# A decoder layer's output projection: norms two column steps sooner, the FFN's last input norm inside its first unit, the table load behind the first down weights

## The chip, the cores and the metric

The kernel runs on one core of a Trainium2 chip. The time is that of one execution on the device, in microseconds (us); before and after are compared by medians over several executions.

## The reference

One decoder layer over 2048 prompt tokens and 32 sample tokens (2080 columns), in float32, D_MODEL 1024, D_FF 2688. The part that bears on the change is the end of the layer:

```python
    merged = jnp.concatenate([_rmsnorm(attn, p['g_attn']), _rmsnorm(ssm, p['g_ssm'])], axis=-1)
    x = x + merged @ p['w_out']
    f, conv_new = _conv_ffn(_rmsnorm(x, p['norm_ffn']), conv_prev,
                            p['w_up'], p['conv_w'], p['conv_b'], p['w_down'])
    x = x + f

def _conv_ffn(h, prev, w_up, conv_w, conv_b, w_down):
    L = h.shape[1]
    up = h @ w_up
    buf = jnp.concatenate([prev.astype(up.dtype), up], axis=1)
    c = conv_b + sum(conv_w[i] * buf[:, i:i + L] for i in range(CONV_W))
    a, g = jnp.split(c, 2, axis=-1)
    return (jax.nn.silu(g) * a) @ w_down, buf[:, -(CONV_W - 1):]
```

A final rmsnorm follows. `_rmsnorm` scales each token by the inverse root of its mean square, and by a weight per channel.

## The kernel before, in words

Channels lie on the partitions, tokens along the free axis. A float32 product is computed as three matmuls on two halves of each operand: `split` (L81) casts the high half on ScalarE (ACT) and subtracts it for the low half on VectorE (DVE) or GpSimd (POOL); `mm3` (L90) multiplies high by high, low by high and high by low (L92 to L94). Names that end in h and l are those halves.

*Output projection* (stage "wo"). `TILES3` cuts the columns into eight tiles of 260, numbered `it`. In each, eight output blocks `m` are made of 24 matmuls of 260 columns. A block's residual is loaded into a tile `xm` (12 buffers), DVE adds the PSUM sum to it (L1160), and it is written to the scratch `x2scr`. Four PSUM banks ("mm") hold block sums, two ("st") hold statistics. Between the blocks stand the norms of the tiles on either side. `merged_sums` loads the next tile's attention and SSM outputs (`mt`) and sums their squares; `merged_norm` makes its normalised halves mh and ml, by way of `mf` (two buffers, DVE), ACT's cast and POOL's subtraction. `rstd` (L97) does the scale: a matmul with ones (st_m, st_f), Ln and Exp on ACT, and three operations on DVE (L107 to L110). After block 2, `ffn_norm` normalises the tile before for the FFN: eight DVE products (L1128) into `h2` (three buffers), each written to the scratch `h2scr`. `early_sums` in tiles 5 and 6 and `begin_ffn` prepare FFN inputs from it.

*FFN.* It runs in two groups of columns (gi 0 and 1) of 21 units (j). A unit multiplies two up-weight blocks with the group's inputs x0, t2, q1 and q0 in 168 matmuls of 262 columns, as products ux, u2, s2, u3, s3, u4, s1: some sums are formed ahead of the product (q1, t2 and q0 are such sums of inputs), and some partial sums serve two outputs, for which ACT copies the running bank (`ca`, `cb`) before TensorE adds on. `conv` does the depthwise convolution and the gate, and writes the result `cc` to `actscr`. After a group's units stands `down` (L1419), the down projection in column tiles `TILESD`: `load_a` loads halves ah and al from `actscr`, `load_wd` (L1399) the raw weights wdr (four buffers), which are split into wdh and wdl. `prepare(1)` splits the second group's inputs beside the first `down`; `finish` and `last_norm` do the final rmsnorm.

*What sets the order.* TensorE's (PE) order is that of the code (`manual_schedule`). The other engines' order is made by a scheduler at build time. All loads and stores are issued by SyncE (SP) in one queue, in order. `after_preload` (L641) puts the ACT table load for Ln and Exp at a place in ACT's order, and holds back what is written inside it until that load; the FFN's Silu uses another table. Before, the whole of `down` stands inside one.

Of the kernel before, what the change touches and what calls it, by code (L numbers as in the profile page):

```python
# [18 lines left out]
P = 128  # L19
# [608 lines left out]
def body(tc, a):  # L628
# [16 lines left out]
    with ExitStack() as top:  # L645
# [399 lines left out]
        for tok in ORDER.split():  # L1045
            if tok == "Y":
                after_s5()
            elif tok == "T":
                steps["g"] = start_glu()
            elif tok == "M":  # L1050
                with after_preload():
                    st.norm = merged_norm(0, *st.sums, PS, "w")
                    st.ms_close()
            elif tok == "A":
                psw_close()
                psa_close()
                psg, psg_close = psum("p2pg", 4)
                st.glups = psg
                att_close()
                kvp_close()  # L1060
                ha, ha_close = pool("fha", "left")
                wop, wo_close = pool("wo", "left")
                for m in range(3, KD):
                    load_wo(m, wop, *[(nc.scalar, nc.vector, nc.gpsimd)[e] for e in WOE[m - 3]])
            else:
                next(steps[tok])
# [47 lines left out]
        with after_preload():  # L1114
            st.gl2_close()
            st.gl_close()
            p3b, p3b_close = pool("p3b", "left")
            st.p3o = p3b
            stg, stg_close = pool("stg", "left", 2)
# [3 lines left out]
            def ffn_norm(it, xs, ss):  # L1123
                t0, n = TILES3[it]
                r = rstd(c, p3b, pst, "st", ss, n, ones[1024], f"f_{it}")
                for k in range(KD):
                    h = p3b.tile([P, n], F32, tag="h2", name=f"h2_{it}_{k}", bufs=3)
                    nc.vector.scalar_tensor_tensor(h, xs[k], g_ffn[:, k : k + 1], r, ALU.mult, ALU.mult)  # L1128
                    nc.sync.dma_start(h2scr[:, k, t0 : t0 + n], h)

            def begin_ffn():
# [8 lines left out]
                for sub in range(2):  # L1140
                    t2 = ffn.t2[sub] = hi_lo(ffn.hc, [4, W], f"t2{sub}", 0)
                    for k in range(0, 4, 2):
                        s = ffn.c2.tile([P, 2, W], F32, tag="c2", name=f"t2r_{sub}_{k}")
                        nc.sync.dma_start(s, t2scr[:, sub, k : k + 2])
                        split(nc, *[t[:, k : k + 2] for t in t2], s, nc.scalar, (nc.vector, nc.gpsimd)[k // 2])

            old = None
            for it, (t0, n) in enumerate(TILES3):
# [5 lines left out]
                for m in range(KD):  # L1154
# [7 lines left out]
                    xs.append(xm)  # L1162
                    if it + 1 < len(TILES3):
                        if m == 0:
                            sums = merged_sums(it + 1, p3m)
                        if m == 3:
                            nxt = merged_norm(it + 1, *sums, pst, "st")
                    if m == 2 and old is not None:
# [5 lines left out]
                old = (it, xs, sumsq(c, p3b, xs, n, f"f_{it}", nc.vector))  # L1174
            ffn_norm(*old)
        ps_close()
        pst_close()
        psj_close()


        sp, up, c2 = ffn.sp, ffn.up, ffn.c2
        p3b_close()
        wo_close()
        hb, hb_close = pool("fhb", "left")
        xp, xp_close = pool("fxo", "left")
        psx, psx_close = psum("fpx", 4)
        psu, psu_close = psum("fpu", 2)
        psv, psv_close = zip(*[psum(f"fpv{i}", 1) for i in range(2)])

# [9 lines left out]
        def load_sums(gi, sub):  # L1199

            q1, t2 = ffn.q1[sub], ffn.t2[sub] = hi_lo(hb, [2, 4, W], f"q1{sub}", gi), hi_lo(ffn.hc, [4, W], f"t2{sub}", gi)
            for k in range(4):
# [15 lines left out]
        def load_wup(gi, j):  # L1218

            lo_eng = nc.vector if gi == 0 and j == 0 else nc.gpsimd  # L1220
            raws = []
# [29 lines left out]
        def load_q(i):  # L1251
            for sub in range(2):
                q = (ffn.q0, ffn.q1)[i][sub] = hi_lo(hb, [2, 4, W], f"q{i}{sub}", 0)
                for k in range(4):
                    s = c2.tile([P, 2, W], F32, tag="c2", name=f"q{i}r_{sub}_{k}")
                    nc.sync.dma_start(s, qscr[:, sub, i, k])
                    split(nc, *[t[:, :, k] for t in q], s, nc.scalar, (nc.gpsimd, nc.vector)[k % 2])

# [119 lines left out]

        def finish(t0, n, xs):

            ss = sumsq(c, DP, xs, n, f"fo_{t0}", nc.vector)
            yield
# [16 lines left out]
        def load_wd(gi, j, t0):  # L1399
# [5 lines left out]
            if gi and j < 14:  # L1405
                if j in (4, 5):
                    w = [ffn.hc.tile([P, D], F32R, tag=f"t2{j - 4}{i}", name=f"wd{i}_{j}") for i in "hl"]
                else:
                    i = j if j < 4 else j - 6
                    pl, nm = ((ha, "x0"), (hb, "q1"), (hb, "q0"))[0 if j < 4 else 1 + i // 4]  # L1410
                    t = pl.tile([P, 2, D], F32R, tag=f"{nm}{i % 4 // 2}{'hl'[i % 2]}", name=f"wd_{j}")
# [7 lines left out]
        def down(gi, beside):  # L1419

            old = None
            for ti, (t0, n) in enumerate(TILESD[gi]):
# [18 lines left out]
                for i, j in enumerate(order):  # L1441
                    for ahead in range(i, min(i + 3, NF)):
                        if ahead not in hls:
# [19 lines left out]
                for m in range(KD):  # L1463
# [3 lines left out]
                    with tc.high_priority(offset=HPD):  # L1467
                        nc.vector.tensor_tensor(x, x, pts[m][:, :n], ALU.add)  # L1468
                old = finish(t0, n, xs)
                next(old)  # L1470
# [10 lines left out]
        def last_norm():  # L1481
            with after_preload():
                next(old, None)

        old = None
        for gi in range(2):
            for j in range(NF):
                if (gi, j) != (0, 0):
                    ws = load_wup(gi, j)
                unit(gi, j, ws, None if j else last_norm if gi else lambda: load_q(0))  # L1490
            with after_preload():
                beside = prepare(1) if gi == 0 else iter(())
                old = down(gi, beside)
                for _ in beside:
                    pass
                if gi:
                    next(old, None)
        nc.sync.dma_start(a["o_tail"][:, :, 0:2], tailp)
        xp_close()
        hb_close()  # L1500
        ha_close()
        ffn.hc_close()
        ffn.c2_close()
# [117 lines left out]
```

## Time and profile before

| | us |
|---|---|
| median of 3 executions (lowest to highest) | 2224.45 (2221.5 to 2226.35) |
| the profiled execution | 2223.61 |
| its span in the profile | 2221.8 |
| TensorE busy | 2067.9 (93%) |
| DVE, POOL, ACT busy | 1330.2, 1192.1, 1058.9 |

The profiled execution was granted a mean TensorE clock of 0.965 of full speed. In the profile's rows L12 is line 12 of the kernel. A timeline row has the start and the length in us, engine, line, operation and tiles, written from source to target with "<-"; a bracket at its end is the idle time ahead of it on that engine and what ended it. A row of a group has the count, the busy time in us and the mean in ns of one, and the idle time ahead. A DMA row has the transfer, the count, its size and the median time in us from issue to landing.

### The profile page before, as it was taken

The page shows a single profiled execution, that of the slowest core. Times are in us where ns is not written, and L with a number is a line of the kernel's source. Part 1 is how long each engine was busy: PE and PEld are TensorE (multiplying, and loading weights), DVE is VectorE, ACT ScalarE, POOL GpSimd, SP SyncE. Part 2 cuts the span into 40 slices and gives each one's busy share as a digit, 9 for nine tenths or more (in the row PEclk, how much of TensorE's full clock was granted, in tenths as well). Part 3 has the DMA queues.
Part 4 walks back from the last instruction along what each step waited for, and adds up shares of the span by engine and source line. Part 5 has one row for each costly group of instructions (what it writes and reads, how often), then busy time and mean ns, then how long its engine had stood idle before and what let it go on. Part 6 is the DMA issues. An engine that isn't in the chain of part 4 may idle for free.

```text
span 2221.8 us, 41548 instructions
## 1 busy us (share of the span) xinstructions
PE 2067.9 (93%) x14685; PEld 1933.8 (87%) x14685; DVE 1330.2 (60%) x3328; ACT 1058.9 (48%) x2459; POOL 1192.1 (54%) x1166
## 2 busy tenths in 40 slices
PE   8969999978998979999999899999999999899997
PEld 7967878857988979999999687788999999888997
DVE  8859898457567766676667532417666666601231
ACT  6525554674443356666666432225556656532111
POOL 4857776334454456666665453555666666372211
PEclk9979999989999879999999899999999999999999
DMA  7855434685577752333333684844233333393643
GB/s 233 252 148 156 123 108 129 128 239 157 170 225 229 237 185 90 116 108 104 102 108 112 215 291 153 284 154 153 96 109 108 97 105 106 107 260 129 202 132 97
DMA packets 294352, 347.59 MB, mean 156 GB/s; under 512 B 42344, under 2 KB 250864, under 8 KB 294128
## 3 DMA queue, kind: packets, MB, share of 16 engines
q1 hardware_dynamic: 294144, 344.94, 51.1%
q8 instruction: 116, 1.90, 0.4%
q14 instruction: 92, 0.75, 0.1%
HBM read 232.70 MB, written 107.80 MB: 153 GB/s over the span
## 4 chain that ended last, share of the span: by engine, by line
PE 73%; DVE 7%; DMA 6%; issue 6%; POOL 3%; ACT 3%; SPq 2%; DVEq 0%; POOLq 0%; ACTq 0%
PE ux L1317 21%; PE u L1317 16%; PE dn L94 7%; PE dn L93 7%; PE dn L92 7%; PE qkv L92 2%; PE qkv L94 1%; PE qkv L93 1%; SPq L776 1%; PE o L541 1%; PE tp_b L530 1%; POOL ml L87 1%; PE wo L93 1%; PE wo L94 1%; PE wo L92 1%
## 5 line engine op out<-in xcount | busy, mean ns | idle before, releaser
L87 POOL TENSOR_TENSOR wdl<-wdr,wdh 128x1024 fp32r<-128x1024 f32 x65 | 159.7, 2464 | 270.3 <-ACT wdh L84 263.6
L92 PE MATMUL dn<-ah,wdh 128*128 128x512 f32 (+3 forms) x552 | 204.5, 370 | 15.0 <-ACT wdh L84 10.7
L94 PE MATMUL dn<-ah,wdl 128*128 128x512 f32 (+3 forms) x552 | 204.8, 371 | 3.2 <-POOL wdl L87 3.2
L93 PE MATMUL dn<-al,wdh 128*128 128x512 f32 (+3 forms) x552 | 204.6, 371 | 0.5 <-DMA al<-actscr 0.5
L1468 DVE TENSOR_TENSOR xo<-xo,dn 128x512 f32<-128x512 f32 (+3 forms) x40 | 21.9, 584 | 302.2 <-PE dn L94 302.1
L1282 ACT ACTIVATE cc<-u,cw 128x260 f32<-128x260 f32 (+1 forms) x252 | 141.5, 563 | 98.4 <-DVE u L1356 68.9
L84 ACT CAST wdh<-wdr 128x1024 fp32r<-128x1024 f32 x65 | 68.0, 1049 | 232.1 <-PE dn L93 208.9
L87 POOL TENSOR_TENSOR wls<-s,whs 128x1024 fp32r<-128x1024 f32 x41 | 98.8, 2411 | 133.4 <-ACT whs L84 133.4
L1283 DVE SCALAR_TENSOR_TENSOR cc<-u,cw,cc 128x260 f32<-128x260 f32 (+1 forms) x252 | 120.8, 480 | 62.4 <-ACT cc L1282 61.0
L93 PE MATMUL wo<-ml,wo 128*128 128x260 f32 x512 | 150.9, 295 | 7.2 <-POOL ml L87 7.0
L92 PE MATMUL wo<-mh,wo 128*128 128x260 f32 x512 | 152.2, 297 | 2.2 <-ACT mh L84 2.2
L94 PE MATMUL wo<-mh,wo 128*128 128x260 f32 x512 | 149.1, 291 | 0.0
L92 PEld LDWEIGHTS dn<-ah,wdh 128*128 128x128 f32 x552 | 104.7, 190 | 33.3 <-ACT wdh L84 11.3
L1356 DVE TENSOR_TENSOR u<-u,cb 128x262 f32<-128x262 f32 x84 | 36.4, 434 | 159.0 <-PE u L1317 159.0
L92 PE MATMUL qkv<-hh_p,wqh 128*128 128x256 f32 (+1 forms) x384 | 114.4, 298 | 12.1 <-DVE vs L879 8.2
L94 PEld LDWEIGHTS dn<-ah,wdl 128*128 128x128 f32 x552 | 104.5, 189 | 21.4 <-POOL wdl L87 5.1
L87 POOL TENSOR_TENSOR wlt<-s,wht 128x512 fp32r<-128x512 f32 x41 | 53.0, 1292 | 127.2 <-ACT wht L84 65.5
L93 PEld LDWEIGHTS dn<-al,wdh 128*128 128x128 f32 x552 | 104.8, 190 | 17.8 <-DMA al<-actscr 1.0
L1284 DVE SCALAR_TENSOR_TENSOR cc<-u,cw,cc 128x260 f32<-128x260 f32 (+1 forms) x252 | 119.4, 475 | 0.8
L87 POOL TENSOR_TENSOR wlg<-wur,whg 128x1024 fp32r<-128x1024 f32 x41 | 98.7, 2407 | 25.6 <-ACT whg L84 25.6
L93 PE MATMUL qkv<-hl_p,wqh 128*128 128x256 f32 (+1 forms) x384 | 111.0, 289 | 0.0
L94 PE MATMUL qkv<-hh_p,wql 128*128 128x256 f32 (+1 forms) x384 | 110.8, 289 | 0.0
(573 smaller groups left out, 8367.6 us busy)
## 6 DMA issues: line engine op xcount, KB each, us to landing
actscr<-cc SPq DMA_DIRECT2D x168, 260.0 KB, 4.7
wur<-in_w_up SPq DMA_DIRECT2D x84, 512.0 KB, 3.3
wdr<-in_w_down SPq DMA_DIRECT2D x77, 512.0 KB, 5.2
x<-in_xT SPq DMA_DIRECT2D x56, 256.0 KB, 3.8
hs<-h2scr SPq DMA_DIRECT2D x44, 262.0 KB, 4.9
ah<-actscr SPq DMA_DIRECT2D x42, 256.0 KB, 3.8
al<-actscr SPq DMA_DIRECT2D x42, 256.0 KB, 4.6
mt<-mscr SPq DMA_DIRECT2D x16, 520.0 KB, 5.3
```

The lines of the kernel that those rows point to most:

```text
L84: nc.scalar.copy(hi, src)
L87: lo_eng.tensor_tensor(lo, src, hi.bitcast(F32), ALU.subtract)
L92: nc.tensor.matmul(ps, w[0], x[0], start=first, stop=False)
L93: nc.tensor.matmul(ps, w[0], x[1], start=False, stop=False)
L94: nc.tensor.matmul(ps, w[1], x[0], start=False, stop=last)
L530: nc.tensor.transpose(tp[:, P * j : P * j + P], ss[kv][:, j, P * ch : P * ch + P], c.ident)
L541: nc.tensor.matmul(o_ps[64 * kv : 64 * kv + 64, :], vt[:, 64 * kv : 64 * kv + 64], pts[kv, ch], start=(ch == 0), stop=(ch == 1))
L1282: nc.scalar.activation(cp, pp[:, 2:], AF.Identity, bias=w[3], scale=w[2])
L1283: nc.vector.scalar_tensor_tensor(cp, pp[:, 1 : npr + 1], w[1], cp, ALU.mult, ALU.add)
L1284: nc.vector.scalar_tensor_tensor(cp, pp[:, 0:npr], w[0], cp, ALU.mult, ALU.add)
L1317: nc.tensor.matmul(pt[:, :W], x[p][:, k], y[q][:, k], start=start and k + i == 0, stop=k == 3 and i == 2, skip_group_check=True)
L1356: v.tensor_tensor(c21[s], c21[s], cb[s][:, 0], ALU.add)
```

## The change

It does four things. `merged_norm` is called after block 1 of a tile (block 3 in tile 0) and `merged_sums` after block 5 of the tile before that. `ffn_norm` writes in place into `xm` and has no h2 tiles. The last `ffn_norm`, some pools and the loading of q0 stand in a function `finish_front`, which runs in the middle of unit (0,0); q1 has a pool of its own (`hd`), and DVE makes all low halves of t2 and q1, POOL those of the first unit's weights. And `down` no longer stands inside `after_preload`: only the first tile's final sums of squares do. ah and al are loaded four ahead instead of three.

```diff
-            p3b, p3b_close = pool("p3b", "left")
-            st.p3o = p3b
+            st.p3o, p3o_close = pool("p3o", "left")
...
                 for k in range(KD):
-                    h = p3b.tile([P, n], F32, tag="h2", name=f"h2_{it}_{k}", bufs=3)
+                    h = xs[k]
                     nc.vector.scalar_tensor_tensor(h, xs[k], g_ffn[:, k : k + 1], r, ALU.mult, ALU.mult)
                     nc.sync.dma_start(h2scr[:, k, t0 : t0 + n], h)
...
                     xs.append(xm)
-                    if it + 1 < len(TILES3):
-                        if m == 0:
-                            sums = merged_sums(it + 1, p3m)
-                        if m == 3:
-                            nxt = merged_norm(it + 1, *sums, pst, "st")
+                    if m == 0 and it == 0:
+                        sums = merged_sums(1, p3m)
+                    if m == (1 if it else 3) and it + 1 < len(TILES3):
+                        nxt = merged_norm(it + 1, *sums, pst, "st")
+                    if m == 5 and it + 2 < len(TILES3):
+                        sums = merged_sums(it + 2, p3m)
                     if m == 2 and old is not None:
...
-            ffn_norm(*old)
         ps_close()
...
+        hd, hd_close = pool("fhd", "right")
         psx, psx_close = psum("fpx", 4)
         psu, psu_close = psum("fpu", 2)
-        psv, psv_close = zip(*[psum(f"fpv{i}", 1) for i in range(2)])
+
+        def finish_front():
+
+            nonlocal hb, xp, psv, hb_close, xp_close, psv_close
+            with after_preload():
+                ffn_norm(*old)
+            pst_close()
+            p3b_close()
+            hb, hb_close = pool("fhb", "left")
+            xp, xp_close = pool("fxo", "left")
+            psv, psv_close = zip(*[psum(f"fpv{i}", 1) for i in range(2)])
+            load_q(0)
+
+        hb = xp = psv = hb_close = xp_close = psv_close = None
...
-            q1, t2 = ffn.q1[sub], ffn.t2[sub] = hi_lo(hb, [2, 4, W], f"q1{sub}", gi), hi_lo(ffn.hc, [4, W], f"t2{sub}", gi)
+            q1, t2 = ffn.q1[sub], ffn.t2[sub] = hi_lo(hd, [2, 4, W], f"q1{sub}", gi), hi_lo(ffn.hc, [4, W], f"t2{sub}", gi)
...
-            lo_eng = nc.vector if gi == 0 and j == 0 else nc.gpsimd
+            lo_eng = nc.gpsimd
...
-                q = (ffn.q0, ffn.q1)[i][sub] = hi_lo(hb, [2, 4, W], f"q{i}{sub}", 0)
+                q = (ffn.q0, ffn.q1)[i][sub] = hi_lo((hb, hd)[i], [2, 4, W], f"q{i}{sub}", 0)
                 for k in range(4):
                     s = c2.tile([P, 2, W], F32, tag="c2", name=f"q{i}r_{sub}_{k}")
                     nc.sync.dma_start(s, qscr[:, sub, i, k])
-                    split(nc, *[t[:, :, k] for t in q], s, nc.scalar, (nc.gpsimd, nc.vector)[k % 2])
+                    split(nc, *[t[:, :, k] for t in q], s, nc.scalar, nc.vector if i else (nc.gpsimd, nc.vector)[k % 2])
...
-                    for ahead in range(i, min(i + 3, NF)):
+                    for ahead in range(i, min(i + 4, NF)):
...
-            with after_preload():
-                next(old, None)
-
-        old = None
+            next(last, None)
+
         for gi in range(2):
             for j in range(NF):
                 if (gi, j) != (0, 0):
                     ws = load_wup(gi, j)
-                unit(gi, j, ws, None if j else last_norm if gi else lambda: load_q(0))
-            with after_preload():
-                beside = prepare(1) if gi == 0 else iter(())
-                old = down(gi, beside)
-                for _ in beside:
-                    pass
-                if gi:
-                    next(old, None)
+                unit(gi, j, ws, None if j else last_norm if gi else finish_front)
+            beside = prepare(1) if gi == 0 else iter(())
+            last = down(gi, beside)
+            for _ in beside:
+                pass
+        next(last, None)
```

In the order, SP in tile 4 of the projection: xm_4_4 to xm_4_7 are the residuals of blocks 4 to 7, h2_3 the FFN's input from tile 3.

```order
L1129 DMA h2scr_64<-h2_3_0_9812 128x260
L1129 DMA h2scr_64<-h2_3_1_9815 128x260
L1129 DMA h2scr_64<-h2_3_2_9818 128x260
L1161 DMA x2scr_63<-xm_4_3_9836 128x260
L1156 DMA xm_4_4_9935<-in_xT 128x260
L1156 DMA xm_4_5_9964<-in_xT 128x260
L1129 DMA h2scr_64<-h2_3_3_9821 128x260
L1129 DMA h2scr_64<-h2_3_4_9824 128x260
L1156 DMA xm_4_6_9993<-in_xT 128x260
L1129 DMA h2scr_64<-h2_3_5_9827 128x260
L1156 DMA xm_4_7_10022<-in_xT 128x260
L1156 DMA xm_5_0_10074<-in_xT 128x260
```

```order
L1129 DMA h2scr_64<-xm_3_0_9315 128x260
L1129 DMA h2scr_64<-xm_3_1_9344 128x260
L1129 DMA h2scr_64<-xm_3_2_9443 128x260
L1129 DMA h2scr_64<-xm_3_3_9499 128x260
L1129 DMA h2scr_64<-xm_3_4_9528 128x260
L1129 DMA h2scr_64<-xm_3_5_9557 128x260
L1129 DMA h2scr_64<-xm_3_6_9612 128x260
L1129 DMA h2scr_64<-xm_3_7_9641 128x260
L1156 DMA xm_4_4_9906<-in_xT 128x260
L1156 DMA xm_4_5_9935<-in_xT 128x260
L1156 DMA xm_4_6_9990<-in_xT 128x260
L1156 DMA xm_4_7_10019<-in_xT 128x260
```

The sources of the h2scr writes are now xm tiles, and all eight stand ahead of the load of xm_4_4, which takes the buffer of xm_3_0.

TensorE at the end of the projection and the start of the FFN (wo_7_7 is the last block, st_f_7 the statistics of the last tile, ux, u3 products of unit 0):

```order
L93 MATMUL wo_7_7_11225<-ml_7_6_10766,wo07_8108 128x260
L94 MATMUL wo_7_7_11225<-mh_7_6_10765,wo17_8109 128x260
L92 MATMUL wo_7_7_11225<-mh_7_7_10771,wo07_8108 128x260
L93 MATMUL wo_7_7_11225<-ml_7_7_10772,wo07_8108 128x260
L94 MATMUL wo_7_7_11225<-mh_7_7_10771,wo17_8109 128x260
L101 MATMUL st_f_7_11275<-ss_f_7_11252,ones1024_77 128x260
L1317 MATMUL ux_0_0_0_11407<-x00h_0_8872,whv_0_0_11339 128x262
```

```order
L1328 MATMUL ux_0_0_1_11310<-t21l_0_10908,whs_0_0_11250 128x262
L1328 MATMUL ux_0_0_1_11310<-t21h_0_10907,wls_0_0_11251 128x262
L101 MATMUL st_f_7_11411<-ss_f_7_11199,ones1024_77 128x260
L1328 MATMUL u3_0_0_0_11488<-q10h_0_11263,whs_0_0_11250 128x262
L1328 MATMUL u3_0_0_0_11488<-q10l_0_11264,whs_0_0_11250 128x262
L1328 MATMUL u3_0_0_0_11488<-q10h_0_11263,wls_0_0_11251 128x262
```

The statistics of the last tile stood between the projection and the first unit; now they stand behind 96 matmuls of that unit, ahead of u3, which reads q1.

SP around the start of the second group's `down` (wdr are raw down weights, cc results of the convolution, ah and al its inputs):

```order
L1303 DMA actscr_65<-cc_7_19_24606 128x2x260
L1303 DMA actscr_65<-cc_4_20_24719 128x2x260
L1303 DMA actscr_65<-cc_5_20_24720 128x2x260
L1431 DMA ah_1024_0_24908<-actscr_65 128x448
L1431 DMA al_1024_0_24909<-actscr_65 128x448
L1303 DMA actscr_65<-cc_6_20_24877 128x2x260
L1431 DMA ah_1024_1_24912<-actscr_65 128x448
L1431 DMA al_1024_1_24913<-actscr_65 128x448
```

```order
L1416 DMA wdr_1024_12_25272<-in_w_down 128x1024
L1416 DMA wdr_1024_13_25305<-in_w_down 128x1024
L1314 DMA actscr_65<-cc_4_20_24662 128x2x260
L1314 DMA actscr_65<-cc_5_20_24663 128x2x260
L1416 DMA wdr_1024_14_25338<-in_w_down 128x1024
L1443 DMA ah_1024_0_24850<-actscr_65 128x448
L1314 DMA actscr_65<-cc_6_20_24820 128x2x260
L1443 DMA al_1024_0_24851<-actscr_65 128x448
L1443 DMA ah_1024_1_24854<-actscr_65 128x448
```

Before, three weight loads were issued by then; now fifteen stand ahead of the first ah, the last of them behind two of the last unit's cc writes.

More of the change, by code (lines that the diff above doesn't have):

```diff
@@ L1061, in body @@
                 ha, ha_close = pool("fha", "left")
+                p3b, p3b_close = pool("p3b", "left")
                 wop, wo_close = pool("wo", "left")
@@ L1144, in begin_ffn @@
                         nc.sync.dma_start(s, t2scr[:, sub, k : k + 2])
-                        split(nc, *[t[:, k : k + 2] for t in t2], s, nc.scalar, (nc.vector, nc.gpsimd)[k // 2])
+                        split(nc, *[t[:, k : k + 2] for t in t2], s, nc.scalar, nc.vector)
             old = None
@@ L1174, in body @@
                 old = (it, xs, sumsq(c, p3b, xs, n, f"f_{it}", nc.vector))
-            ffn_norm(*old)
         ps_close()
-        pst_close()
         psj_close()
         sp, up, c2 = ffn.sp, ffn.up, ffn.c2
-        p3b_close()
+        p3o_close()
         wo_close()
-        hb, hb_close = pool("fhb", "left")
-        xp, xp_close = pool("fxo", "left")
+        hd, hd_close = pool("fhd", "right")
         psx, psx_close = psum("fpx", 4)
         psu, psu_close = psum("fpu", 2)
-        psv, psv_close = zip(*[psum(f"fpv{i}", 1) for i in range(2)])
+        def finish_front():
[9 more added lines that the diff above has]
+        hb = xp = psv = hb_close = xp_close = psv_close = None
         def stages(gi, sub, k, nm):
@@ L1377, in tile, with finish @@
                 return dt(shape, dtype, name)
-        def finish(t0, n, xs):
-            ss = sumsq(c, DP, xs, n, f"fo_{t0}", nc.vector)
+        def finish(t0, n, xs, first):
+            with after_preload() if first else nullcontext():
+                ss = sumsq(c, DP, xs, n, f"fo_{t0}", nc.vector)
             yield
@@ L1409, in load_wd @@
                     i = j if j < 4 else j - 6
-                    pl, nm = ((ha, "x0"), (hb, "q1"), (hb, "q0"))[0 if j < 4 else 1 + i // 4]
+                    pl, nm = ((ha, "x0"), (hd, "q1"), (hb, "q0"))[0 if j < 4 else 1 + i // 4]
                     t = pl.tile([P, 2, D], F32R, tag=f"{nm}{i % 4 // 2}{'hl'[i % 2]}", name=f"wd_{j}")
@@ L1468, in down @@
                         nc.vector.tensor_tensor(x, x, pts[m][:, :n], ALU.add)
-                old = finish(t0, n, xs)
+                old = finish(t0, n, xs, ti == 0)
                 next(old)
@@ L1501, in body @@
         ha_close()
+        hd_close()
         ffn.hc_close()
```

## The prediction

> **What bounds the kernel now.** I read the busy shares first, then the windows around the three places that the change touches, then the timeline of TensorE there with the bracket at each row's end (idle time ahead of it, and what ended it).
>
> ```profile
> span 2221.8 us, 41548 instructions
> PE 2067.9 (93%) x14685; PEld 1933.8 (87%) x14685; DVE 1330.2 (60%) x3328; ACT 1058.9 (48%) x2459; POOL 1192.1 (54%) x1166
> ```
>
> TensorE is busy for 93% of the span, no other engine for more than 60%. The changed kernel issues the same matmuls, so only TensorE's idle time and low-clock time can move. Below, each row is a stretch, its length, busy time of PE, weight loads, DVE, ACT and POOL, the granted clock, the DMA share and GB/s.
>
> ```profile
> 549.60:776.60 227.00, 211.08 (x1580) 202.81 (x1578) 153.78 (x331) 93.99 (x234) 104.70 (x126) 0.95 0.69 212
> 776.60:821.60 45.00, 29.87 (x170) 27.58 (x170) 27.66 (x48) 19.76 (x40) 21.69 (x15) 0.73 0.61 199
> 669.00:681.00 12.00, 9.98 (x80) 9.54 (x79) 9.31 (x23) 3.21 (x8) 3.19 (x5) 1.00 0.77 249
> 717.00:729.00 12.00, 10.19 (x52) 9.01 (x51) 5.79 (x13) 5.78 (x16) 8.35 (x11) 0.72 0.87 253
> ```
>
> The output projection (first row) loses little per tile; its boundary to the FFN (second row) has 15.1 of 45 us idle, at a clock of 0.73. On TensorE, the projection:
>
> ```profile
> 586.43 0.38 PE L101 MATMUL st_f<-ss_f,ones 128*128 128x260 f32 x1
> 617.88 0.46 PE L101 MATMUL st_m<-ss_m,ones 128*128 128x260 f32 x1 [1.97 <-DVE t_f L107]
> 664.73 0.28 PE L94 MATMUL wo<-mh,wo 128*128 128x260 f32 x1
> 664.85 0.28 PE L92 MATMUL wo<-mh,wo 128*128 128x260 f32 x1
> 674.40 0.46 PE L101 MATMUL st_m<-ss_m,ones 128*128 128x260 f32 x1 [2.02 <-DVE t_f L107]
> 749.44 0.39 PE L93 MATMUL wo<-ml,wo 128*128 128x260 f32 x1 [1.06 <-POOL ml L87]
> 761.64 0.38 PE L101 MATMUL st_f<-ss_f,ones 128*128 128x260 f32 x1
> ```
>
> The first and last st_f stand in tiles 1 and 7: six tiles in 175.2 us, 29.2 each. One matmul starts 0.12 us after the other, so 192 take 23.04, and three statistics matmuls some 0.45 each make 24.4. Thus 4.8 us are lost per tile, 28.8 in six: a wait of about 2.0 for the statistics' DVE work (two of the rows show it), small ones for ml at a tile's start, and clock dips. Then the boundary and the starts of the down projection:
>
> ```profile
> 781.97 0.80 PE L101 MATMUL st_f<-ss_f,ones 128*128 128x260 f32 x1 [5.36 <-DVE ss_f L122]
> 794.15 0.39 PE L1317 MATMUL u<-q10h,whs 128*128 128x262 f32 x1 [1.00 <-ACT q10h L84]
> 800.07 0.58 PE L1317 MATMUL u<-q10l,whs 128*128 128x262 f32 x1 [5.52 <-POOL q10l L87]
> 811.27 0.39 PE L1317 MATMUL u<-q00l,whg 128*128 128x262 f32 x1 [1.91 <-POOL q00l L87]
> 821.78 0.28 PE L1317 MATMUL ux<-x00h,whv 128*128 128x262 f32 x1
> 1242.83 0.79 PE L92 MATMUL dn<-ah,wdh 128*128 128x512 f32 x1 [9.73 <-ACT wdh L84]
> 1245.27 0.80 PE L94 MATMUL dn<-ah,wdl 128*128 128x512 f32 x1 [1.22 <-POOL wdl L87]
> 1945.38 0.74 PE L92 MATMUL dn<-ah,wd 128*128 128x448 f32 x1 [9.26 <-ACT wd L84]
> 1947.83 0.74 PE L94 MATMUL dn<-ah,wd 128*128 128x448 f32 x1 [1.33 <-POOL wd L87]
> ```
>
> Four brackets of the boundary add to 13.8 us; the first down matmuls cost 10.95 and 10.59.
>
> **The change part by part.** The sum stands against the profiled execution, 2223.61 us; the median shown is 0.84 above it, added at the end.
>
> *Output projection.* The next tile's norm now starts after block 1, so its ml are done before the tile begins; the tile-start waits and the st_m wait go. Late next is the residual. ffn_norm writes into xm, and blocks 4 to 7 of a tile reuse the buffers that the tile before filled with blocks 0 to 3. So their loads wait for writes of h2scr, and in SP's order stand behind all eight.
>
> ```profile
> 646.14 0.48 ACT L103 ACTIVATE ln_m<-st_m,eps 128x260 f32<-128x260 f32 x1 [0.83 <-PE st_m L101]
> 646.65 0.42 ACT L105 ACTIVATE r_m<-ln_m 128x260 f32<-128x260 f32 x1
> L975 DVE SCALAR_TENSOR_TENSOR mf<-mt,vec,rs_m 128x260 f32<-128x260 f32 x56 | 30.1, 573 | 3.5 <-POOL ml L87 3.4
> L1128 DVE SCALAR_TENSOR_TENSOR h<-xm,vec,rs_f 128x260 f32<-128x260 f32 x64 | 34.5, 574 | 6.8 <-DMA h2scr<-h 6.4
> 676.55 0.54 SPq L1129 DMA_DIRECT2D h2scr<-h  x1
> xm<-in_xT SPq DMA_DIRECT2D x63, 130.0 KB, 2.9
> h2scr<-h SPq DMA_DIRECT2D x54, 130.0 KB, 3.5
> ```
>
> Two blocks take 48 × 0.12 = 5.8 us; with a statistics matmul (about 0.45), Ln and Exp the scales stand near 7.1. DVE then does 19 operations before the first h (three times three for the scales, eight mf, two additions to xm), at 0.5 to 0.573 us: 16.6 to 18.0. Eight h by 0.574 and the issue of the last write (0.54) reach 21.7 to 23.1; a load lands 2.9 later, 24.6 to 26.0 into the tile. TensorE needs the PSUM bank that block 4's addition frees at 23.04, where the next tile begins. That is a wait of 1.6 to 3.0 per tile; I take 2.7 in a mean tile, since in tiles 4 to 6 the loads that prepare the FFN share DVE and SP. Six tiles lose 16. For clock dips I keep 5 of the 12.8 that now are neither an st_m wait (2.0 each, 12 in six tiles) nor ml waits of about 4: 21 against 28.8, **−8**. Bounds: a wait of 1.0 and no dips, with 6 × 0.9 for the rest, loses 11.4 (−17); a wait of 5.3 per tile beside dips of 5 loses 36.8 (+8).
>
> A rule of the Trainium skill, "TensorE: Matmul & The Clock Gate", Part 1 (the HAM clock gate), says that the clock is halved only after an idle window of about 3.4 us and returns after as long a busy one. By it waits under 3.4 us cost only themselves, my 5 us of dips would go, and an estimate for this term would be −13. The trace only half agrees: 669 to 681, which holds the wait of 2.02, was granted 1.00, but 717 to 729 got 0.72 with none of the long waits quoted here. I stay with the rows.
>
> *Boundary.* The last ffn_norm moves into unit (0,0), behind two products that need only x0 and t2, which were made earlier. The wait of 5.36 goes, and q1, loaded early and split on DVE, no longer makes TensorE wait 5.52. Before, tile 7 began at 776.6 − 23.0 = 753.6, and the unit ended at 821.8, 68.2 later. After: the last block-4 load lets the unit start near 24.4; two products of 11.5 us end at 35.9 at the pitch above; ca waits about 2 behind q1's casts on ACT, and u3's second half about 1.5 for the statistics. u3's 48 matmuls (5.8) reach 45.2. u4 needs q0, which is split after the last h2scr write: the scales near 37.4, eight h by 0.574, and 3.5 until the write lands, 45.5; four more for the first cast and split put u4's start near 49.4, where it was at 57.7 before (811.27). From there the unit takes some 10 as before, to about 59: **−9**. Bounds: all four brackets gone, −13; q1's and the ca wait as long as q10l's 5.52 and 1.00 were together, −3.
>
> *Down start, group 0.*
>
> ```profile
> 1240.44 1.28 ACT L643 ACT_TABLE_LOAD   x1
> 1235.82 0.44 SPq L1431 DMA_DIRECT2D ah<-actscr  x1
> 1244.28 1.49 DVE L87 TENSOR_TENSOR x00l<-hs,x00h 128x524 fp32r<-128x524 f32 x1 [3.40 <-ACT x00h L84]
> al<-actscr SPq DMA_DIRECT2D x6, 256.0 KB, 4.4
> ```
>
> The table load leaves the path (−1.3), and the first weights are ready early. But splits like x00l now precede u4's eviction on DVE: three or four by 1.49 push the last cc from 1240.0 to about 1241. On SP a weight load and the cc writes stand ahead of the first ah, which goes from 1235.82 to about 1243; al is issued behind it and lands 4.4 later, 1248. TensorE starts at 1248 against 1245.27 from which it ran freely: **+3**. Bounds: all of 1.28 and the 1.22 gained without a delay, −2; two splits more, +6.
>
> *Down start, group 1.*
>
> ```profile
> 1920.30 0.36 ACT L1331 COPY ca<-ux 128x262 f32<-128x262 f32 x1
> 1922.11 1.29 POOL L87 TENSOR_TENSOR wlt<-s,wht 128x512 fp32r<-128x512 f32 x1 [3.09 <-ACT tailp L1286]
> 1938.18 0.41 SPq L1431 DMA_DIRECT2D ah<-actscr  x1
> 1942.99 1.28 ACT L643 ACT_TABLE_LOAD   x1
> 1945.41 2.37 POOL L87 TENSOR_TENSOR wd<-wdr,wd 128x1024 fp32r<-128x1024 f32 x1 [22.00 <-ACT wd L84]
> ```
>
> POOL's 22.00 idle us are now filled with low halves of the weights. SP's order puts the load of weights 14, whose raw buffer (four) comes free when wd_10 is split, ahead of the first ah. Splits begin near 1921; wlt (1.29) and eleven by 2.37 end near 1948.4, with 1 to 1.5 for the wait on the last ca, 1949.4. So ah goes from 1938.18 to 1949.4, al behind one cc write to 1951.5, landing by 4.4 at 1955.9, against 1947.83: **+8**. In the middle of the unit a wd cast ahead of the ca copy may move it from 1920.3 to 1922.7, and TensorE stalls 1.3 there, which is under the +10 of the upper bound. Lower bound: POOL two splits quicker and no stall, +3. Weights waited for nothing after 1947.83 before, so early ones return nothing.
>
> *Rest.* The pools opened earlier, the first unit's low halves on POOL, last_norm without a table load and ah four ahead instead of three cost 0: the low halves stand in the boundary, where POOL was busy 21.7 of 45 us; the other edits beside matmuls that wait for nothing. A microsecond each way if that cover is gone.
>
> Sum: −8 −9 +3 +8 = −6: 2217.6 on the profiled run's scale, 2218.4 on the median's.
>
> **The rivals.** *Slower: the residual's loads.* Where the wait behind the h2scr writes makes a tile lose 6.0 us, the projection costs 7.2 more than before: sum +9.2, 2234. Zero sum is at 4.5 per tile, a clear slowdown from 5.2. For: all eight writes stand ahead of the load, and DVE is busy 154 of 227 us there. Against: with dips of 0.8 per tile, 6.0 needs the load to land at 28.2, over two us later than my upper chain. *Much faster: SP isn't in the way.* Should ah go out as early as before, the starts lose only the table load and the wait for the first low half (1.28 + 1.22, 1.28 + 1.33), and the sum is −8 −9 −2.5 −2.6 = −22: 2202. Against it speaks that ah stands behind weight loads in SP's order; for it, that those wait for POOL alone, whose splits may begin earlier than 1921. *No change.* Half of projection and boundary (−8.5) beside +3 and +8 gives +2.5: 2227; with +3 and +5 for the starts, 2224.
>
> **How the numbers follow.** About 0.2%, 4.4 us, is what a measurement of this kernel can tell from no change: faster is below 2220.0, slower above 2228.9. Forecast 0.50, slow loads 0.20, much faster 0.17, no change 0.13. Faster is the much faster case and 0.35 of the forecast, 0.52; same is the no-change case and 0.13 of the forecast, 0.26; slower is the slow loads and the last 0.02, 0.22. The range leaves out half of each outer case, 2203 to 2232; the forecast alone spans 2211 to 2226.
>
> **What would show it.** Right: no bracket of about 2 us ahead of st_m; st_f between tiles 1 and 7 in about 167 us; a wait for DVE's xm addition at tile starts; unit (0,0) ending some 59 us after tile 7 began; the second down start near 10 us idle on a DMA of al. Wrong: tile-start waits of 5 us (the first rival), or down matmuls that start at once behind the last unit (the second). A clock below 0.9 in the projection would void the dips that I kept.

## The result and the profile after

The changed kernel takes 2244.2 us in the median (2241.67 to 2249.62, four executions) where the kernel before takes 2222.97: 1.0104 of it, with a 95% interval of 1.007 to 1.0139. It is slower by some 21 us; 2218.4, in a range from 2203 to 2232, was forecast. The profiled execution took 2243.47 us, with this span:

```profile
span 2241.7 us, 41507 instructions
PE 2059.5 (92%) x14685; PEld 1931.3 (86%) x14685; DVE 1352.0 (60%) x3326; ACT 1055.4 (47%) x2459; POOL 1195.8 (53%) x1168
```

TensorE issues the same 14685 matmuls, so the two traces can be laid side by side by the start of each stage's first matmul. The table gives the time from one such start to the next; its last line is the difference at the last TensorE instruction.

| stretch | before | after | forecast | measured |
|---|---|---|---|---|
| up to tile 1 of the projection | 577.8 | 576.9 | 0 | −0.9 |
| tile 1 to tile 7 (six tiles) | 168.8 | 180.2 | −8 | +11.4 |
| tile 7 to unit (0,2) | 95.8 | 91.8 | −9 | −4.0 |
| last unit of group 0 to the 49th down matmul | 45.8 | 50.0 | +3 | +4.2 |
| rest of that down, two units of group 1 | 287.2 | 290.2 | 0 | +3.0 |
| last unit of group 1 to the 49th down matmul | 44.3 | 52.0 | +8 | +7.7 |
| rest of the last down | 252.6 | 250.6 | 0 | −2.0 |
| all, with the units between | | | −6 | +19.7 |

The first two forecasts were worked out between other marks: −8 between the st_f of tiles 1 and 7, where 175.2 us became 181.6 (+6.4), and −9 from there to unit (0,1), where 60.1 became 56.7 (−3.5). Unit (0,1), for which nothing was forecast, took 24.3 us instead of 20.6.

The windows of the six tiles, before and after (length, busy time of PE, weight loads, DVE, ACT, POOL, clock, DMA share, GB/s):

```profile
577.80:746.60 168.80, 157.64 (x1190) 151.59 (x1189) 115.00 (x258) 69.99 (x180) 80.78 (x98) 0.96 0.71 215
```

```profile
576.90:757.10 180.20, 156.01 (x1190) 153.68 (x1189) 136.37 (x260) 69.55 (x182) 87.46 (x103) 0.93 0.63 194
```

DVE's instructions are about as many, and it is busy for 21 us more. TensorE in the changed kernel, at tile starts and in the first two units:

```profile
634.97 0.56 PE L92 MATMUL wo<-mh,wo 128*128 128x260 f32 x1 [4.79 <-DVE xm L1160]
695.65 0.36 PE L92 MATMUL wo<-mh,wo 128*128 128x260 f32 x1 [3.82 <-DVE xm L1160]
726.16 0.56 PE L92 MATMUL wo<-mh,wo 128*128 128x260 f32 x1 [4.45 <-DVE xm L1160]
757.11 0.56 PE L92 MATMUL wo<-mh,wo 128*128 128x260 f32 x1 [4.17 <-DVE xm L1160]
787.19 0.36 PE L1328 MATMUL ux<-x00h,whv 128*128 128x262 f32 x1 [1.72 <-DVE xm L1160]
795.02 0.39 PE L1328 MATMUL ux<-t20h,whs 128*128 128x262 f32 x1 [1.74 <-ACT ca L1342]
802.88 0.59 PE L1328 MATMUL u<-q10h,whs 128*128 128x262 f32 x1 [2.73 <-DVE t_f L107]
811.56 0.39 PE L1328 MATMUL u<-q00h,whg 128*128 128x262 f32 x1 [1.07 <-ACT q00h L84]
816.11 0.59 PE L1328 MATMUL u<-q00l,whg 128*128 128x262 f32 x1 [4.16 <-POOL q00l L87]
829.74 0.39 PE L1328 MATMUL u<-x00h,whv 128*128 128x262 f32 x1 [2.01 <-DVE cc L1313]
```

The 2.0 us ahead of st_m are gone, as forecast; in their place each tile from tile 2 on starts with 2.8 to 4.8 us of waiting for the addition to xm. The one chain behind 695.65, in the tile that began at 664.83, on DVE:

```profile
677.66 0.89 DVE L975 SCALAR_TENSOR_TENSOR mf<-mt,vec,rs_m 128x260 f32<-128x260 f32 x2
...
686.00 5.75 DVE L1128 SCALAR_TENSOR_TENSOR xm<-xm,vec,rs_f 128x260 f32<-128x260 f32 x8
...
695.09 0.75 DVE L1160 TENSOR_TENSOR xm<-xm,wo 128x260 f32<-128x260 f32 x2
```

and on SP's queue:

```profile
686.58 5.69 SPq L1129 DMA_DIRECT2D h2scr<-xm  x8
692.32 2.85 SPq L1156 DMA_DIRECT2D xm<-in_xT  x6
```

The first mf stands 12.8 us into the tile, the first h at 21.2, the last h ends at 26.9, the residuals are issued at 27.5 and the first addition runs at 30.3, where TensorE wanted the bank at about 27. At the two down starts, TensorE and SP of the changed kernel:

```profile
1255.62 0.80 PE L92 MATMUL dn<-ah,wdh 128*128 128x512 f32 x1 [14.58 <-DMA ah<-actscr]
1937.03 0.39 PE L1328 MATMUL ux<-t20h,whs 128*128 128x262 f32 x1 [1.59 <-ACT ca L1342]
1968.91 0.74 PE L92 MATMUL dn<-ah,wd 128*128 128x448 f32 x1 [16.97 <-DMA ah<-actscr]
```

```profile
1250.42 0.54 SPq L1443 DMA_DIRECT2D ah<-actscr  x1
...
1941.14 19.05 SPq L1416 DMA_DIRECT2D wdr<-in_w_down  x9
...
1962.57 0.49 SPq L1443 DMA_DIRECT2D ah<-actscr  x1
```

Weights no longer end these waits, ah does, and it stands behind the wdr loads in the queue.

### The profile page after: what moved, and what is told of

It is laid out like the page before. It is cut to its first block, busy times and chain, and to the rows that moved or that the text cites. A ratio compares the mean times of both kernels' runs of the same rounds, so it can differ in the third digit from the quotient of the medians.

```text
span 2241.7 us, 41507 instructions
## 1 busy us (share of the span) xinstructions
PE 2059.5 (92%) x14685; PEld 1931.3 (86%) x14685; DVE 1352.0 (60%) x3326; ACT 1055.4 (47%) x2459; POOL 1195.8 (53%) x1168
## 4 chain that ended last, share of the span: by engine, by line
PE 70%; DVE 11%; DMA 6%; issue 4%; ACT 3%; POOL 3%; SPq 2%; DVEq 0%; POOLq 0%; ACTq 0%
PE ux L1328 20%; PE u L1328 15%; PE dn L93 7%; PE dn L94 7%; PE dn L92 7%; DVE xm L1128 2%; PE qkv L92 1%; PE qkv L93 1%; PE qkv L94 1%; SPq L776 1%; PE wo L92 1%; PE wo L94 1%; PE wo L93 1%; PE o L541 1%; PE tp_b L530 1%
## 5 line engine op out<-in xcount | busy, mean ns | idle before, releaser
L92 PE MATMUL dn<-ah,wdh 128*128 128x512 f32 (+3 forms) x552 | 205.1, 372 | 19.7 <-DMA ah<-actscr 16.7
L1480 DVE TENSOR_TENSOR xo<-xo,dn 128x512 f32<-128x512 f32 (+3 forms) x40 | 21.9, 584 | 306.0 <-PE dn L94 305.9
L92 PE MATMUL wo<-mh,wo 128*128 128x260 f32 x512 | 153.5, 300 | 25.8 <-DVE xm L1160 25.8
L92 PEld LDWEIGHTS wo<-mh,wo 128*128 128x128 f32 x512 | 102.9, 201 | 27.5 <-issue 24.6
L92 PE MATMUL dn<-ah,wd 128*128 128x448 f32 (+2 forms) x288 | 94.7, 329 | 23.2 <-DMA ah<-actscr 19.5
```

What stands on the lines that cost most here:

```text
L92: nc.tensor.matmul(ps, w[0], x[0], start=first, stop=False)
```

## The experiments

Twelve kernels ran. For each this table has the differences to the trace of before in the same stretches (us; six tiles as their length), and its time as a ratio to before.

| run | six tiles | tile 7 to (0,2) | down 0 | first units of group 1 | down 1 | ratio (95%) |
|---|---|---|---|---|---|---|
| changed | 180.2 | −4.0 | +4.2 | +1.8 | +7.7 | 1.0104 (1.007 to 1.0139) |
| e1 | 168.3 | −3.2 | +5.0 | +1.7 | +9.6 | 1.0051 (1.0032 to 1.0069) |
| e2 | 186.0 | −6.2 | +0.5 | −1.1 | −0.2 | 1.0051 (1.0034 to 1.0069) |
| e3 | 185.7 | −10.1 | +4.4 | +2.9 | +8.5 | 1.009 (1.0056 to 1.0124) |
| e4 | 181.7 | −4.8 | +0.1 | −1.1 | −0.5 | 1.0068 (1.005 to 1.0086) |
| e5 | 172.9 | −5.9 | −0.5 | −0.1 | 0.0 | 0.999 (0.9976 to 1.0004) |
| e6 | 167.4 | −8.9 | +0.4 | −1.0 | −0.6 | 0.9969 (0.9954 to 0.9984) |
| e7 | 166.5 | −0.9 | +0.2 | −1.0 | −0.3 | 0.9992 (0.9979 to 1.0005) |
| e8 | 167.9 | −1.9 | −4.9 | −1.1 | −4.0 | 0.9946 (0.9925 to 0.9967) |
| e9 | 179.0 | −6.3 | +4.8 | +1.9 | +7.7 | 1.011 (1.0078 to 1.0143) |
| e10 | 177.4 | −4.8 | +4.5 | +2.5 | +8.2 | 1.0125 (1.0094 to 1.0156) |
| e11 | 169.0 | −7.6 | −4.7 | −1.0 | −3.8 | 0.9939 (0.9919 to 0.9958) |
| e12 | 167.3 | −7.5 | −4.1 | −0.8 | −4.2 | 0.9945 (0.9923 to 0.9967) |

Pairs with the same front (changed and e4, e6 and e11, e7 and e8) differ by 1.4 to 1.6 us in the six tiles; less than that is not read as an effect.

**e1, the norms back in the changed kernel.**

```diff
-                    if m == (1 if it else 3) and it + 1 < len(TILES3):
+                    if m == 3 and it + 1 < len(TILES3):
                         nxt = merged_norm(it + 1, *sums, pst, "st")
```

(and merged_sums of the next tile at block 0 again.)

> The changed kernel with merged_sums and merged_norm back at blocks 0 and 3, all else as changed. Theory (W): the norms of the next tile now stand ahead of ffn_norm on DVE, and because ffn_norm writes in place, blocks 4 to 7's residuals wait for its eight stores; with the norms back behind ffn_norm the waits for DVE's xm addition at tile starts (2.8 to 4.8 us each) go, those for ml and st_m come back, and tile 1's start to tile 7's start takes about 169 us (before 168.8, changed 180.2): some 2233 us. Rival (I): writing in place alone delays the residuals; then 175 us or more with the same waits on the addition: 2239 or more.

Six tiles took 168.3 us, the median was 2232.64: theory W's numbers. In-place writing stays in this kernel and, with the norms at block 3, costs nothing that shows in these six tiles. The old wait is back:

```profile
615.12 0.46 PE L101 MATMUL st_m<-ss_m,ones 128*128 128x260 f32 x1 [2.38 <-DVE t_f L107]
```

**e2, the early norms alone in the kernel before.** The same lines the other way round, with h2 tiles.

> The kernel before with the earlier norms alone; h2 tiles of their own stay. Theory W: a residual waits for DVE's reading of xm alone, not for stores, but three h2 buffers still tie the reading to the stores; small waits of 0 to 2 us per tile, six tiles in 163 to 170 us: 2216 to 2224. Rival (E): the early norms by themselves are what delays the residuals: six tiles in about 180, 2233.

Rival E held, and W's second half fell: 186.0 us, 5.8 more than in the changed kernel. At five of the six tile starts TensorE waits for the same addition to xm (1.20 to 7.14 us), and twice for a late st_f (4.47 and 2.96).

```profile
662.45 0.56 PE L92 MATMUL wo<-mh,wo 128*128 128x260 f32 x1 [4.44 <-DVE xm L1160]
727.71 0.56 PE L92 MATMUL wo<-mh,wo 128*128 128x260 f32 x1 [7.14 <-DVE xm L1160]
```

In tiles 2 to 6 of this run the first h starts 21.9 to 28.7 us into the tile (before 15.3 to 21.4), and the residuals' loads are issued from 24.6 to 31.0. So the order on DVE costs the time: the next tile's norms ahead of this tile's h, whatever h is written to. Stores are not out of it here either, as three writes of h2scr stand ahead of the loads in SP's queue. Writing in place makes them eight: the load goes out 6.3 us behind the first h in the changed kernel's tile quoted above, 3.1 us in this run's tile 2. Why h start later still here than in the changed kernel stays open.

**e3, ffn_norm ahead of the norms, both at block 1.**

```diff
+                    if m == 1 and old is not None:
+                        ffn_norm(*old)
                     if m == (1 if it else 3) and it + 1 < len(TILES3):
...
-                    if m == 2 and old is not None:
-                        ffn_norm(*old)
```

> The changed kernel with ffn_norm of the tile before moved from block 2 to block 1, ahead of the next tile's norms; all else as changed. Theory W: eight h end some 6 us earlier on DVE than now (mf stand behind them), the residual of block 4 lands near 20 us into the tile, the waits on xm's addition go, and the norms are still ready: six tiles in 150 to 160 us, 2217 to 2224. Rival: ml is late instead, the waits turn up as ml or mh at the tiles' starts, six tiles at 170 or more: 2233 or more.

The theory missed. The rival's numbers came, 185.7 us and 2241.01, but not for its reason. In the six tiles the additions to xm hold nothing up any more, and ml costs 0.5 us once; the third statistics matmul waits (1.3 to 6.0 us), since there are two PSUM banks for them and the first is free when DVE has read it.

```profile
614.37 0.77 PE L101 MATMUL st_m<-ss_m,ones 128*128 128x260 f32 x1 [5.28 <-DVE t_f L107]
741.88 0.77 PE L101 MATMUL st_m<-ss_m,ones 128*128 128x260 f32 x1 [5.98 <-DVE t_f L107]
```

**e4, down as before in the changed kernel.** The four lines on `after_preload` around `down` and in `last_norm` are restored, and `i + 4` is `i + 3`.

> The changed kernel with down and last_norm inside after_preload again and three loads ahead. Theory: the two down starts cost +4.1 and +7.7 us against before, the first unit of group 1 +1.8, 2.3 come back late; undone, the first down's idle time is about 10.9 us (now 14.6) and the second's 10.6 (now 17.6 with al), and no 1.6 wait for ca in the last unit: 2232 to 2235. Rival: the later starts were absorbed by what follows; 2241 or more.

2234.3 us, as expected, and both starts are those of before to 0.5 us; the first:

```profile
1252.08 0.80 PE L92 MATMUL dn<-ah,wdh 128*128 128x512 f32 x1 [9.73 <-ACT wdh L84]
1254.52 0.80 PE L94 MATMUL dn<-ah,wdl 128*128 128x512 f32 x1 [1.22 <-POOL wdl L87]
```

Beside it, the first units of group 1 go from +1.8 to −1.1.

**e5 and e6, from the kernel before: ffn_norm at block 1, and the norms at block 3 or 2.**

```diff
+                    if m == 1 and old is not None:
+                        ffn_norm(*old)
                     if it + 1 < len(TILES3):
...
-                        if m == 3:
+                        if m == (2 if it else 3):
                             nxt = merged_norm(it + 1, *sums, pst, "st")
-                    if m == 2 and old is not None:
-                        ffn_norm(*old)
```

(e5 has the move of ffn_norm alone, with the norms at block 3.)

> The kernel before with ffn_norm alone moved from block 2 to block 1; the next tile's norms stay at block 3. Theory (Q): what costs is which queue stands ahead: next-tile norms ahead of ffn_norm on DVE delay the residuals (changed kernel, and the kernel before with early norms), and three statistics matmuls close together wait for their two PSUM banks (ffn_norm first, norms also at block 1). With ffn_norm at block 1 and the norms two blocks later neither holds: the wait of 2.0 to 2.7 for t_f ahead of st_m goes, six tiles take 156 to 165 us (before 168.8): 2209 to 2219. Rival (D): DVE as a whole is what limits a tile, so any order gives 168 or more: 2220 or more.

172.9 us, 2223.29: theory Q missed and D held. The st_m wait did go; waits for ml (up to 1.92) and ss_f (2.33 once) are in its place.

> The kernel before with ffn_norm at block 1 and the next tile's norms at block 2 (block 3 in tile 0). Theory Q: the wait ahead of st_m stays at about 2 us (one block between the statistics, as before), those for ml at the tiles' starts (0.5 to 1.2) go: six tiles in 160 to 169 us. Rival D: 168 or more, as in the kernel before.

167.4 us, in Q's range but not clear of D's bound by more than the wobble; e11, with the same order, took 169.0. The wait ahead of st_m is larger than before:

```profile
726.42 0.77 PE L101 MATMUL st_m<-ss_m,ones 128*128 128x260 f32 x1 [3.59 <-DVE t_f L107]
```

What this order gains lies in tile 7 and the boundary (−8.9): tile 7 takes 27.5 us to the first unit (before 36.0), its ml waits are gone and the wait for the last sum of squares is 3.56 (before 5.36). The median is 2216.29.

**e7, the changed kernel with norms at block 3, ffn_norm at block 1, down as before, and the last statistics 48 matmuls sooner.**

```diff
+            if mid and not gi:
+                mid()
             p2 = banks((psu, psu), "u2", "u2")
...
-            if mid:
+            if mid and gi:
                 mid()
```

> The changed kernel with norms back at block 3, ffn_norm at block 1, the last tile's statistics 48 matmuls sooner in unit (0,0) (behind its first product), and down as before. Theory: six tiles as in the run with ffn_norm at block 1, 156 to 165 us; in unit (0,0) u3 no longer waits for t_f (2.7) nor u4 for q0's low half (2 to 4), so tile 7's start to unit (0,2) takes 85 to 89 us (before 95.8, changed 91.8): 2200 to 2212. Rival: q0's path is bound by DVE and the stores, wherever the statistics stand: 91 or more, 2213 or more.

Missed twice: 166.5 us, and the boundary 94.9 instead of 85 to 89; the median is 2222.5. The sooner ffn_norm puts eight h ahead of the unit's convolution on DVE, and u4 needs the bank that the convolution reads:

```profile
803.87 0.56 PE L1327 MATMUL u<-q00h,whg 128*128 128x262 f32 x1 [7.38 <-DVE cc L1294]
```

**e8, two weights early.** Against e7, the main lines:

```diff
-            with after_preload():
+            for j in range(2):
+                early[TILESD[gi][0][0], j] = load_wd(gi, j, TILESD[gi][0][0])
+            with tc.issue_after(st.lastcc):
                 beside = prepare(1) if gi == 0 else iter(())
                 last = down(gi, beside)
```

(`st.lastcc` is the last unit's last cast; the table load stands in `finish`, as in the changed kernel.)

> As the run before it, but the first two down weights of each group may be cast and split among the last unit's steps, and everything else of down follows the last unit's last cast; the table load stands behind the first down tile. Theory: what cost in the changed kernel is the first ah behind the weight loads in SP's queue, and not weights split early as such; with ah where it was, the idle time at the two starts falls from 10.9 and 10.6 us to 6 to 9 each, 4 to 8 us faster than the run before it. Rival: splits among the last unit's steps hold back the last cc and so ah; 10 us or more each, same time or slower.

2214.87 us, 7.6 under e7. The starts wait for ah, but now after a short idle time, and nothing waits behind them:

```profile
1240.26 0.80 PE L92 MATMUL dn<-ah,wdh 128*128 128x512 f32 x1 [7.05 <-DMA ah<-actscr]
1917.61 0.39 PE L1327 MATMUL ux<-t20h,whs 128*128 128x262 f32 x1 [1.59 <-ACT ca L1341]
1937.41 0.74 PE L92 MATMUL dn<-ah,wd 128*128 128x448 f32 x1 [4.88 <-DMA ah<-actscr]
```

The second start is below the 6 to 9 us expected. The changed kernel's idea is right here, and its order on SP's queue was what it paid for.

**e9 and e10, GpSimd's sums taken away from beside h.** Groups of h on DVE in one window of before, of the changed kernel and of e10:

```profile
L1128 DVE SCALAR_TENSOR_TENSOR h<-xm,vec,rs_f 128x260 f32<-128x260 f32 x48 | 23.7, 526 | 2.6 <-DMA h2scr<-h 2.3
```

```profile
L1128 DVE SCALAR_TENSOR_TENSOR xm<-xm,vec,rs_f 128x260 f32<-128x260 f32 x48 | 35.5, 807 | 0.0
```

```profile
L1128 DVE SCALAR_TENSOR_TENSOR xm<-xm,vec,rs_f 128x260 f32<-128x260 f32 x48 | 25.6, 601 | 0.0
```

```diff
+            if it >= 2:
+                return mt, [sumsq(c, p3, mt[4 * h : 4 * h + 1], n, f"m{h}_{it}", nc.gpsimd) for h in range(2)]
```

> The changed kernel with three of four squares and all of GpSimd's additions left out of merged_sums for tiles 2 to 7 (the sums of squares that the norms use are incomplete). Theory (C): those additions now run while DVE makes ffn_norm's h; 41 of 49 h overlap GpSimd work and take 0.86 us, those alone 0.42. With them gone the mean h of tiles 1 to 6 falls from 0.81 to at most 0.60 us, each residual comes 2 to 4 us sooner, six tiles take 160 to 172 us (changed 180.2). Rival (O): order alone delays the residuals, and ml subtractions overlap h anyway; h stays at 0.7 or more and six tiles at 176 or more.

The end of one line changes:

```diff
-  f"m{h}_{it}", nc.gpsimd) for h in range(2)]
+  f"m{h}_{it}", nc.vector if it >= 2 else nc.gpsimd) for h in range(2)]
```

> The changed kernel with merged_sums' additions for tiles 2 to 7 on DVE instead of GpSimd; nothing is left out. Theory C: six additions of about 0.42 us are added to DVE per tile and GpSimd no longer runs beside h; h falls to at most 0.60 us, which outweighs the additions: six tiles in 166 to 176 us. Rival O: DVE has 2.5 us more per tile in front of h or of the additions to xm: six tiles at 182 or more.

The mechanism of C was there, its price was not. h fell from 0.807 to 0.621 and 0.601 us, close to what was expected, but the six tiles only to 179.0 and 177.4: rival O's side in e9, between the two in e10. A h alone takes 0.48 us, not the 0.42 of the expectation, and 21 and 19 of 48 h still overlap GpSimd's work, mostly the subtractions of the norms. Of the 11.4 us the collisions with the sums carry 1 to 3, not clear of the wobble. The rest comes with the norms' place (e1 and e2), and how much of it is DVE's order and how much the collisions left was not separated. Neither kernel is faster than the changed one.

**e11 and e12, the best of both on the kernel before:** e6's order and e8's weights; e12 with e10's sums on DVE.

> The kernel before with ffn_norm at block 1, the norms at block 2, and two down weights early with the table load behind the first down tile. Theory: the gains add, since they lie in different stages: 8 to 9 us from the projection's end as in the run with these norms, 7 to 9 us from the two down starts: 2204 to 2210. Rival: the projection's gain was of that one profile: 2212 to 2217.

2208.57 us, 0.9939 of before. By stages the gains of e6 and e8 add (−7.6 at the boundary, −4.7 and −3.8 at the down starts); in the ratio the intervals of e8, e11 and e12 overlap, so none of them is shown to be the fastest.

> As the run before it, with merged_sums' additions for tiles 2 to 7 on DVE. Theory C: in this order GpSimd's sums overlap few h (before: 13 of 48), so there is little to gain and 2.5 us of DVE work per tile to pay; six tiles 1 to 8 us longer than in the run before it: 2206 to 2216. Rival: collisions cost here too, and it is 2 us or more faster than that run.

2207.47 us. The six tiles are 1.7 us shorter, not 1 to 8 longer, and the intervals of the two runs overlap: whether these sums cost anything on GpSimd in this order stays open.

## Why the prediction was wrong

**The projection, −8 forecast, +11.4 measured: the step that failed.** The chain was named with its right links (mf, then h, then the stores, then the residuals' loads), and it was mis-sized at three terms.

First, "the scales stand near 7.1", and the first h at 16.6 to 18.0. In tile 1 they did: the first h began 17.3 us into it. But from tile 2 on the first mf began at 10.5 to 12.8 (8.9 in tile 1) and the first h at 20.3 to 21.7. The estimate took a tile that starts clean, and the wait feeds itself: behind it TensorE runs for a stretch at half clock, so that st_m stands 7.4 to 8.1 us into tiles 2 to 6 and 5.8 into tile 1. What else holds mf back differs from tile to tile. In tile 4, which began at 664.83, the scale on ACT stands behind a square of xm, and that waits for an addition that DVE makes behind FFN inputs. The half-clock stretch and that square:

```profile
666.20:669.60 3.40, 3.40 (x18) 3.40 (x17) 1.66 (x5) 0.59 (x2) 0.00 (x0) 0.51 0.81 236
```

```profile
675.31 0.42 ACT L121 ACTIVATE sq_f<-xm 128x260 f32<-128x260 f32 x1 [2.01 <-DVE xm L1160]
```

Second, h was priced at 0.574 us from a group in which few ran beside GpSimd; beside its sums, in the new place, they took 0.807. Eight of them are 1.9 us longer.

Third, the loss to start from. The 175.2 us stand between two st_f that lie at different places of their tiles, 8.6 us into tile 1 and 15.0 into tile 7. From start to start these six tiles took 168.8 us before, and lost 3.7 each instead of 4.8. The 2.0 us ahead of st_m, counted six times, stood in two of the six tiles, the two of the rows shown. So there was less to win: the working's own 24.4 per tile and 21 of loss make 167.4 us, 1.4 below 168.8 and not 8.

The forecast's wait of 2.7 us in a mean tile was 3.9 (2.79, 4.79, 3.52, 3.82, 4.45 and 4.17). So the rival "the residual's loads" is what happened, with 6.0 us lost per tile as its price: 180.2 us are 30.0 per tile, 5.6 over the 24.4 worked out. Its mechanism was half right. Eight h2scr stores ahead of the load are not needed for it (e2 has three); the norms ahead of h are.

The dips kept in the sum (5 us) were right to keep, and too few: 180.2 less 146.4 for the matmuls and 23.5 of these waits leaves 10. The first wait, and a window with it that has a clock of 0.83 over 10 us, which is 3.4 us at half of it:

```profile
604.11 0.36 PE L92 MATMUL wo<-mh,wo 128*128 128x260 f32 x1 [2.79 <-DVE xm L1160]
```

```profile
601.00:611.00 10.00, 7.21 (x48) 7.03 (x47) 5.00 (x13) 2.94 (x6) 0.57 (x2) 0.83 0.77 214
```

The Trainium skill, "TensorE: Matmul & The Clock Gate", Part 1 (the HAM clock gate), has a window of about 3.4 us, and the length of this dip agrees with it; that an idle time must be as long to bring it on is not what this row shows.

**The boundary, −9 forecast, −4.0 measured.** The waits of 5.36 and 5.52 went, and q1 is early, as said. Unit (0,0) was to end 59 us after tile 7 began and ended at 67.5 (before 75.2, as tile 7 began at 746.6 and not at 753.6). Tile 7 took 30.1 of these, with waits of 2.26 and 1.72 for additions to xm, where 24.4 were worked out. The unit took 37.4, where 34.6 were. The working had a slip here, and so has the section on the change: 72 matmuls stand ahead of st_f, not 96, and "two products" were three products of 24. The last statistics begin at 799.55, u4's low half of q0 comes at 816.11, and this path (scales, eight h, stores, loads, splits) is now what u4 waits for: 1.07 and 4.16. Last, unit (0,1), for which nothing was forecast, waits 2.01 for the convolution that was pushed back, and takes 3.7 us longer than before. e7 shows that an earlier statistics matmul alone does not help, as the h then stand ahead of the convolution.

**The down starts, +3 and +8 forecast, +4.2 and +7.7 measured: right, for the reasons given.** The first ah was forecast at 1243 and 1949.4 and came at 1250.42 and 1962.57, which less the delay at that place (6.7 and 14.0) is 1243.7 and 1948.6. The 1.3 us for ca were 1.59. e4 undoes both, e8 keeps the weights early without the queue in front of ah.

**The rest, 0 forecast, +3.0 measured, 1.8 of it in the first two units of group 1.** The other 1.3 us lie in the rest of the first down, where runs whose down is that of before differ from it by −1.8 to +2.9 (e2, e4 to e7); they are not read as an effect. Each run whose last_norm has no table load shows +1.7 to +2.9 in the first units of group 1 (the changed kernel, e1, e3, e9, e10), each with it −1.1 to −0.1 (the other eight, e8 among them, whose down is not inside after_preload either). The five also share the early weights and the four loads ahead, so it is the trace more than the grouping that points at last_norm. That it was free was wrong, as far as this shows. The last section has the rows.

## What to carry to other kernels

Where an engine takes its work in order, moving one consumer's preparation forward moves everything behind it back; price the work that it overtakes, in the steady state and not in a first round that starts clean. A wait that comes once a round can feed itself, here by a stretch at half clock behind it. And when weights or other bulk loads are made early, look which small load then stands behind them in the queue: at group 1's start two early weights gained 4.0 us where fifteen loads ahead of ah lost 7.7. A loss that is to be won back is read between the same places of two rounds: here two places 6.4 us apart within their tiles made 28.8 us of loss out of 22.4.

## What was not expected of the hardware

An instruction of DVE that starts beside one of GpSimd can last until that one is done. In group 1's first unit, the changed kernel's final scalings take 0.74 us when alone. Below is one alone, one that started beside a GpSimd split, and then that split, which ended at 1527.68:

```profile
1533.60 0.74 DVE L1406 SCALAR_TENSOR_TENSOR xo<-xo,vec,rs_fo 128x512 f32<-128x512 f32 x1
...
1525.36 2.87 DVE L1406 SCALAR_TENSOR_TENSOR xo<-xo,vec,rs_fo 128x512 f32<-128x512 f32 x1
```

```profile
1524.85 2.83 POOL L87 TENSOR_TENSOR wlv<-wur,whv 128x1024 fp32r<-128x1024 f32 x1
```

Without the table load three of the eight scalings were caught in this way (1.44, 2.87 and 2.87), before one (2.87). The unit itself is shorter, 25.8 us instead of 29.8, but the next one waits longer for DVE to release its bank and takes 28.0 instead of 22.2. Its wait before and after:

```profile
1527.77 0.39 PE L1317 MATMUL u<-x00h,whv 128*128 128x262 f32 x1 [1.45 <-DVE cc L1302]
```

```profile
1540.14 0.59 PE L1328 MATMUL u<-x00h,whv 128*128 128x262 f32 x1 [5.73 <-DVE cc L1313]
```

The Trainium skill, "SBUF — State Buffer", under "Who interferes with whom", says that a DVE instruction with two SBUF inputs contends with a GpSimd instruction that reads SBUF, by an exclusive lock, so that the later one waits for the whole of the other. The trace agrees: 2.87 against 0.74. The wait is 5.4 to 5.7 us in the five runs without that table load and 1.4 to 1.5 in the others. That the caught scalings are the whole of the 3 us between the means of the two groups is argued from the trace, and no run took them away by themselves.
